# Key columns of the shared projection by seven-product slabs, the last ones in narrower tiles, and the key norms at the end

## The chip, the cores and the metric

The kernel runs on one core of a Trainium2 chip. TensorE multiplies, VectorE and ScalarE do the elementwise work, GpSimd (POOL) issues loads that add into memory, and SyncE (SP) issues the plain loads. The metric is the device time of one execution in microseconds. The kernel before takes 1988.17 us, the median of three runs (1988.16 to 1988.75).

## The reference

Two decoder layers work on 256 tokens of width 2048, in float32. Between them the kernel makes keys and values that the second layer reads:

```python
kv = rms_norm(x, kv_norm) @ w_kv                     # 2048 x 3072
k1, k2 = kv[..., :768], kv[..., 768:1536]            # two maps of 12 heads x 64
v = kv[..., 1536:]                                   # 12 heads x 128
k1 = partial_rope(rms_norm(k1, k_norm), cos, sin)    # the norm is per head
k2 = partial_rope(rms_norm(k2, k_norm), cos, sin)
```

Each layer also attends to a memory of 256 rows, `mkv = rms_norm(mem, mem_norm[i]) @ w_mem_kv[i]`, with 512 key and 512 value columns. Ahead of the keys and values stands layer 0's feed-forward block, behind them the second layer's input projection (its queries) and the differential attention.

## The kernel before

**Products in three passes.** Float32 operands are split into a rounded high part and a low rest, and a product is high x high, low x high and high x low: three matmuls. Activations are split once for each chunk of 128 features (`split_gain`, line 432: ScalarE writes the high part, VectorE the low one). Weights are split block by block as they come (`Feed._split`, line 190): ScalarE casts a block of 512 columns into one of six slots of `hi_ring` (line 195), VectorE subtracts into the same slot of `lo_ring` (line 198).

**The feed.** A first dry pass of the program writes down the order of all weight blocks; the second pass loads them in that order. A "narrow" job is one such block of 128 x 512. Before TensorE's work of a job is issued, `fill` (line 245) prepares up to three jobs beyond it (`AHEAD`), and loads run a few loads further ahead (`load`, line 129) on the SP queue, into four buffers "raw" of two jobs each (line 138). The instructions of each engine run in order. An engine can also start on instructions that are ready early, so that VectorE and ScalarE may be as far ahead of TensorE as the six slots allow.

**Slabs.** A slab is a pair of feature chunks by 1024 columns, that is a 2 x 2 arrangement of blocks, multiplied with a 2 x 2 arrangement of x (two chunks by two halves of the tokens) by the seven-product scheme of Strassen and Winograd. Each of seven PSUM banks gathers one product over all eight slabs. The left half of the slab is loaded into a tile "slab", the right half beside it; sums of its blocks are made by two adds of VectorE (lines 224 and 238) and by two loads on the POOL queue that add into memory (`add_right`, line 167). A slab has four jobs, which use six, three, six and six matmuls of 512 columns; VectorE makes low halves of 1024, 512, 1024 and 1024 columns for them. The matching sums of x are made by `kv_sums` (line 1588) for each pair of chunks: four VectorE operations of 128 columns, a cast, and a subtraction (line 1605). When a product is complete, `close` (line 1630) combines the banks by two ScalarE copies and seven VectorE adds.

**The clock of the emission.** The program counts ticks: each 128 x 512 job of the tiles ticks once, slab jobs do not. `at(d, fn)` (line 329) puts work `d` ticks later, so other work is spread between the tiles' steps by hand.

**The stage.** After layer 0's feed-forward block the order on TensorE is:
- Three key tiles of 512 columns (`map_tile`, line 500, 16 steps of six matmuls of 512 columns by `wide_step`, line 477). Behind each stand its norms (`key_rows`, line 555: two copies and two squares on ScalarE; two reductions, two multiplications and small operations on VectorE), its rotation (`rope`, line 608) and, nine ticks later, its transposition into `kT` (`turn_rows`, line 635).
- Four tiles of 256 columns on the single bank "st": two for the last 512 value columns, two for the memory's values (`half_step`, line 505: two feature chunks, twelve matmuls of 256 columns). From the second on the slabs of the first 1024 value columns stand between the half steps (`kv_slabs`, line 1612; 26 jobs on 19 half steps once it has begun).
- The memory's key tile (`mk1`, line 1747) with the last two slab jobs. After its seventh step `end` lets the other work go on, and the splits of `x_mx` for the queries are put on the following 16 ticks (line 1755). Behind it come the norms of the memory's keys and copies of its values.
- The query tiles (line 1888), the first of which needs chunk n of `x_mx` at its step n.

Beside this run the squares of the residual (`later_square`, line 747, ticks 2 to 9), the column scales (`columns`, tick 12), the loads of the memory (`mem_again`, line 1558, ticks 8, 17, 26 and 35, into the "raw" buffers of the weights) with four splits each, five to eleven ticks later, and `kv_sums` at ticks 12, 18, ... 54. The chunks of `x_kv` become ready at the end of the feed-forward block; chunk 7 is its last.

Of the kernel before, what the change touches and what calls it, by code (L numbers as in the profile page):

```python
# [311 lines left out]
def program(ctx, tc, plan, dry, xT, memT, par, lam, cst, wst, yT):  # L312
# [192 lines left out]
    def half_step(ps, w, l, c, k, xs):  # L505

        hi, lo = feed.quad([(w, l, k, c, 2), (w, l, k + 1, c, 2)])
# [127 lines left out]
    def turn_rows(raw, i, dst, g, low=None):  # L635


        t4 = pp.tile([P, 2, T], F32, tag="ot"[i // 2 % 2], bufs=1, name="tr")
# [928 lines left out]
    for p in range(4):  # L1567
        at(8 + 9 * p, lambda p=p: mem_again(p))
# [13 lines left out]

    def mv_place(h, n, t):

        four = x_kv[:, 4 * h + 2 * t : 4 * (h + n - 1) + 2 * t + 1 : 4, :]
        return four[:, :, P:T], four[:, :, T + P : 2 * T]
# [22 lines left out]
    for i in range(8):  # L1609
        at(12 + 6 * i, lambda i=i: kv_sums(i))  # L1610

    def kv_slabs():
# [3 lines left out]
        last_v = []  # L1616
# [3 lines left out]
        out = {}  # L1620
# [9 lines left out]
        def close(j):  # L1630
            if j == 0:
                one = tp.tile([P, 2, 512], F32, tag="rows", bufs=3, name="v_a")
                two = tp.tile([P, 2, 512], F32, tag="rows", bufs=3, name="v_b")
                out.update(u=one[:, 0, :], c11=one[:, 1, :], v=two[:, 0, :], c12=two[:, 1, :])
                nc.scalar.copy(out["u"], banks[0])
                add(out["c11"], out["u"], banks[1])
            elif j == 1:
                nc.scalar.copy(out["v"], banks[2])
            elif j == 2:
                u, v, c12 = out["u"], out["v"], out["c12"]  # L1640
                add(u, u, banks[3])
                sub(c12, v, u)
                add(c12, c12, banks[4])
            else:
                u, v = out["u"], out["v"]
                add(u, u, banks[5])
                sub(v, v, u)
                add(u, u, banks[6])
                for k, (c, t, x) in enumerate(
                    ((0, 0, out["c11"]), (1, 0, out["c12"]), (1, 1, v), (0, 1, u))  # L1650
                ):
                    at(1 + k // 2, lambda c=c, t=t, x=x: scale(c, t, x))
# [4 lines left out]
        def run(n, i, j):  # L1657
# [18 lines left out]
            if i == 7:  # L1676
                close(j)
# [3 lines left out]
            for p in range(-1, 9)  # L1681
            for j, i in enumerate((p + 1, p, p, p - 1))
            if 0 <= i < 8
        ]
        slab = {}

        def some(n):
            for _ in range(n):
                i, j = jobs.pop(0)
                if j == 0:  # L1690
                    slab[i] = feed.slab(
                        [
                            [("w_kv", 0, 2 * i, c, 4), ("w_kv", 0, 2 * i + 1, c, 4)]
                            for c in (3, 4)
                        ]
                    )
                run(slab[i], i, j)

        for h in range(4):
            bank = pp.tile([P, 512], F32, tag="st", bufs=1, name="mv1" if h > 1 else "v1")  # L1700
            for q in range(8):
                n = 8 * h + q
                some(0 if n < 9 else 1 if n < 13 else (26 * (n - 12) + 9) // 19 - (26 * (n - 13) + 9) // 19)
                if h < 2:
                    half_step(bank, "w_kv", 0, 10 + h, 2 * q, x_kv)
                else:
                    half_step(bank, "w_mem_kv", 1, h, 2 * q, mems1)
            if h == 0:
                last_v += [tp.tile([P, 512], F32, tag=g, bufs=1, name="v_c") for g in ("acc2", "rowsq")]
            for t in range(2):  # L1710
                two = bank[:, T * t : T * t + T]
                if h < 2:
                    nc.scalar.activation(
                        last_v[t][:, T * h : T * h + T], two, AF.Copy, scale=c1[0][:, t : t + 1]
                    )
                else:
                    two = two.rearrange("p (h d) -> p h d", h=2)
                    split_rows(*mv_place(2 * h - 4, 2, t), two, mem_c[0][:, t : t + 1])
# [298 lines left out]
```

## Time and profile before

| what | value |
|---|---|
| median of three runs | 1988.17 us |
| the profiled execution | 1988.15 us |
| its span, first to last instruction | 1986.4 us |
| TensorE, VectorE, ScalarE, POOL busy | 100%, 91%, 79%, 12% |
| mean granted TensorE clock | 1.000 |
| read from HBM | 422.19 MB, 214 GB/s over the span |

A row of a group reads: line, engine, operation, tile written and tiles read, shapes, count | busy us, mean ns of one | idle time of the engine just before, and what ended it. A row of the timeline begins with start and duration in us. PE is TensorE's matmuls, PEld its weight loads, DVE is VectorE, ACT ScalarE, POOL GpSimd, SPq SyncE's queue.

### The profile page before, as it was taken

To read this page: it belongs to the slowest core of one execution; us is meant where nothing else is said; L and a number is where in the kernel's file an instruction comes from. 1 tells how busy PE (TensorE), PEld (TensorE's weight loads), DVE (VectorE), ACT (ScalarE), POOL (GpSimd) and SP (SyncE) were. 2 spreads that over 40 slices of the span, in tenths; PEclk is the share of its full clock that TensorE was granted. 3 is DMA by queue.
4 is the path that set the end of the run, shared out by engine and by line. 5 is a ranking of instruction groups with operands and counts; after the bars stand their busy time and mean duration, and the time that the engine had idled before them with its cause. 6 is when DMAs were issued, how large, how long until landed. Compare 5 with 4: busy or idle time off the path is not lost.

```text
span 1986.4 us, 32353 instructions
## 1 busy us (share of the span) xinstructions
PE 1982.2 (100%) x10554; PEld 1696.7 (85%) x10554; DVE 1799.4 (91%) x3317; ACT 1566.1 (79%) x2894; POOL 235.3 (12%) x277
## 2 busy tenths in 40 slices
PE   9999999999999999999999999999999999999999
PEld 8888888888888888888898889888888888888888
DVE  8888889999999999889878798989999999999888
ACT  7766677788878888778757799777788888888775
POOL 0000011111111111110011000001111111111110
PEclk9999999999999999999999999999999999999999
DMA  9555578888888888765776534568888888988875
GB/s 316 180 184 198 189 201 236 238 228 234 237 227 236 232 231 231 216 192 193 236 210 204 178 128 139 193 194 231 233 236 230 234 236 224 242 229 229 229 208 146
DMA packets 149929, 426.41 MB, mean 215 GB/s; under 512 B 16896, under 2 KB 19584, under 8 KB 149760
## 3 DMA queue, kind: packets, MB, share of 16 engines
q1 hardware_dynamic: 110448, 353.03, 53.5%
q0 software_dynamic: 39168, 71.32, 21.5%
q8 instruction: 82, 1.34, 0.3%
q14 instruction: 87, 0.71, 0.1%
q10 hardware_dynamic: 144, 0.01, 0.0%
HBM read 422.19 MB, written 2.10 MB: 214 GB/s over the span
## 4 chain that ended last, share of the span: by engine, by line
PE 100%; ACT 0%; DVE 0%; issue 0%
PE x_bank L456 22%; PE x_bank L458 11%; PE p L948 10%; PE p L950 10%; PE p L951 10%; PE wo L456 6%; PE wo L458 3%; PE u L456 2%; PE ff L456 1%; PE u L458 1%; PE q L490 1%; PE k L490 1%; PE q L492 1%; PE q L491 1%; PE k L492 1%; PE k L491 1%
## 5 line engine op out<-in xcount | busy, mean ns | idle before, releaser
L195 ACT CAST hi_ring<-raw 128x512 fp32r<-128x512 f32 x905 | 551.4, 619 | 165.5 <-PE x_bank L456 40.1
L198 DVE TENSOR_TENSOR lo_ring<-raw,hi_ring 128x512 fp32r<-128x512 f32 x905 | 610.2, 686 | 49.2 <-ACT hi_ring L195 42.9
L456 PE MATMUL x_bank<-fx,hi_ring 128*128 128x512 f32 x1728 | 540.1, 394 | 0.0
L458 PEld LDWEIGHTS x_bank<-fx,lo_ring 128*128 128x128 f32 x1728 | 324.5, 188 | 73.5
L198 DVE TENSOR_TENSOR lo_ring<-room,hi_ring 128x1024 fp32r<-128x1024 f32 x256 | 312.6, 1222 | 43.1 <-ACT hi_ring L195 41.6
L195 ACT CAST hi_ring<-room 128x1024 fp32r<-128x1024 f32 x256 | 269.4, 1052 | 95.9 <-PE x_bank L456 44.0
L458 PE MATMUL x_bank<-fx,lo_ring 128*128 128x256 f32 x1728 | 339.5, 278 | 0.0
L456 PEld LDWEIGHTS x_bank<-fx,hi_ring 128*128 128x128 f32 x1728 | 286.3, 189 | 26.0 <-ACT room L835 1.5
L198 DVE TENSOR_TENSOR lo_ring<-slab,hi_ring 128x1024 fp32r<-128x1024 f32 (+1 forms) x272 | 259.4, 954 | 40.2 <-ACT hi_ring L195 36.3
L195 ACT CAST hi_ring<-slab 128x1024 fp32r<-128x1024 f32 (+1 forms) x272 | 224.1, 834 | 61.1 <-PE p L950 28.0
L170 POOL DMA_DIRECT2D slab<-in_w x136 | 117.6, 864 | 1199.9 <-DVE lo_ring L198 1193.6
L948 PE MATMUL p<-hi_ring,sit 128*128 128x512 f32 x480 | 188.3, 392 | 0.0
L950 PE MATMUL p<-hi_ring,sit 128*128 128x512 f32 x480 | 187.4, 391 | 0.0
L951 PE MATMUL p<-lo_ring,sit 128*128 128x512 f32 x480 | 186.6, 389 | 0.0
L170 POOL DMA_DIRECT2D room<-in_w x128 | 110.5, 864 | 485.8 <-DVE lo_ring L198 467.9
L456 PE MATMUL wo<-cat,hi_ring 128*128 128x512 f32 x512 | 161.6, 397 | 0.0
L948 PE MATMUL p<-hi_ring,z 128*128 128x512 f32 x368 | 145.2, 394 | 0.0
L950 PE MATMUL p<-hi_ring,z 128*128 128x512 f32 x368 | 143.8, 391 | 0.0
L951 PE MATMUL p<-lo_ring,z 128*128 128x512 f32 x368 | 143.4, 390 | 0.0
L458 PEld LDWEIGHTS wo<-cat,lo_ring 128*128 128x128 f32 x512 | 95.9, 188 | 22.3
L951 PEld LDWEIGHTS p<-lo_ring,sit 128*128 128x128 f32 x480 | 90.1, 188 | 19.7
L948 PEld LDWEIGHTS p<-hi_ring,sit 128*128 128x128 f32 x480 | 90.0, 187 | 13.1
(464 smaller groups left out, 3671.1 us busy)
## 6 DMA issues: line engine op xcount, KB each, us to landing
raw<-in_w SPq DMA_DIRECT2D x450, 512.0 KB, 4.3
slab<-in_w SPq DMA_DIRECT2D x136, 512.0 KB, 5.7
slab<-in_w POOLq DMA_DIRECT2D x136, 256.0 KB, 5.4
room<-in_w SPq DMA_DIRECT2D x128, 256.0 KB, 4.6
room<-in_w POOLq DMA_DIRECT2D x128, 256.0 KB, 5.5
memraw<-in_mem SPq DMA_DIRECT2D x5, 512.0 KB, 4.7
resid<-in_x SPq DMA_DIRECT2D x8, 256.0 KB, 5.6
out_y<-resid SPq DMA_DIRECT2D x16, 128.0 KB, 1.9
```

The lines of the kernel that those rows point to most:

```text
L170: self.nc.gpsimd.dma_start(t, self.wst[h, :, 0:512], accum_op=ALU.add)
L195: self.last_cast = self.nc.scalar.copy(hi, src)
L198: low = self.nc.vector.tensor_sub(lo, src, hi.bitcast(F32))
L456: nc.tensor.matmul(ps, hi, xs[:, k, :], start=first and c == 0, stop=False)
L458: nc.tensor.matmul(ps[:, T : 2 * T], lo, xs[:, k, 0:T], start=False, stop=last and c == len(ks) - 1,)
L490: nc.tensor.matmul(ps[t], x[t][1], hi, start=k == 0, stop=False)
L491: nc.tensor.matmul(ps[t], x[t][0], hi, start=False, stop=False)
L492: nc.tensor.matmul(ps[t], x[t][0], lo, start=False, stop=k == NK - 1)
L948: nc.tensor.matmul(ps, a[1], hi, start=new, stop=False, **again)
L950: nc.tensor.matmul(ps, a[0], hi, start=False, stop=False, **again)
L951: nc.tensor.matmul(ps, a[0], lo, start=False, stop=end, **again)
```

## The change

It makes one sequence of sixteen slabs: eight for the first 1024 value columns, then eight for the first 1024 key columns, over the same seven banks and the same sums of x. The last 512 key columns come first, as two tiles of 256 columns on "st"; then the last values, then the memory's values. That makes 48 half steps in the place of 48 wide steps and 32 half steps. The slab jobs start at the fifth half step, one for each of six half steps, then 54 on 38; four are left for the memory's key tile. The norms of the last key tile stand at half step 16 (`last_keys`, on raw columns whose scale is put in afterwards), its transposes at half step 24 on bank "st". The products of the values wait in `kv`, and are scaled into `vv` at the end; the key products are combined into "rows" tiles, and `key_rows`, `rope` and the transposes of those two key tiles come 4 to 15 ticks after `end`, which is now called after the eighth step of the memory's key tile. The memory's values wait in four small tiles and are split after that tile. `kv_sums` moves to ticks 1, 5, 8, ... 23, the memory loads to ticks 8, 13, 18 and 23.

```diff
-    def half_step(ps, w, l, c, k, xs):
+    def half_step(ps, blocks, k, xs):
-        hi, lo = feed.quad([(w, l, k, c, 2), (w, l, k + 1, c, 2)])
+        hi, lo = feed.quad(blocks(k) + blocks(k + 1))
...
     for p in range(4):
-        at(8 + 9 * p, lambda p=p: mem_again(p))
+        at(8 + 5 * p, lambda p=p: mem_again(p))
...
     for i in range(8):
-        at(12 + 6 * i, lambda i=i: kv_sums(i))
+        at(2 + 3 * i if i else 1, lambda i=i: kv_sums(i))
+    c1 = []
+    def last_keys(raw):
+        v = tp.tile([P, 16], F32, tag="w16", bufs=6, name="kv")
+        for t in range(2):
+            sq = tp.tile([P, 512], F32, tag="rowsq", bufs=1, name="ksq")
+            nc.scalar.activation(sq, raw[:, t, :], AF.Square, scale=0.125)
+            nc.vector.tensor_reduce(
+                out=v[:, 8 * t : 8 * t + 8], in_=sq.rearrange("p (h d) -> p h d", d=64),
+                axis=AX.X, op=ALU.add,
+            )
...
+            nc.vector.tensor_mul(rows, rows, yb)
+        rope(raw, ktab)
+    def turn_keys(c, i, rows, tag=None):
+        turn_rows(rows, 2 * i, kT[:, 4 * c + 2 * i : 4 * c + 2 * i + 2, :], gcol(G_KN), tag=tag)
...
-        def close(j):
+        def close(g, j):
+            o = (out, keys)[g]
             if j == 0:
...
+                if g:
+                    one = tp.tile([P, 2, 512], F32, tag="rows", bufs=3, name="k_a")
+                    two = tp.tile([P, 2, 512], F32, tag="rows", bufs=3, name="k_b")
...
         jobs = [
             (i, j)
-            for p in range(-1, 9)
+            for p in range(-1, 17)
             for j, i in enumerate((p + 1, p, p, p - 1))
-            if 0 <= i < 8
+            if 0 <= i < 16
         ]
...
+        counts = [0] * 4 + [1] * 6
+        for n in range(38):
+            counts.append((54 * (n + 1) + 9) // 38 - (54 * n + 9) // 38)
+        for n, x in ((16, 2), (24, 3)):
+            while counts[n] < x:
+                m = next(m for m in (n + 2, n - 2, n + 4, n - 4, n + 3, n - 3) if counts[m] == 2)
+                counts[m] -= 1
+                counts[n] += 1
...
+        for h in range(6):
+            left = counts[8 * h]
+            if h == 2:
+                some(1)
+                left -= 1
+                c1.extend(columns("x"))
+                last_keys(k_rows)
+            elif h == 3:
+                for i in range(2):
+                    some(1)
+                    left -= 1
+                    turn_keys(2, i, k_rows, "st")
+            some(left)
+            bank = pp.tile([P, 512], F32, tag="st", bufs=1, name=("k1", "v1", "mv1")[h // 2])
             for q in range(8):
...
+                if q:
+                    some(counts[8 * h + q])
+                half_step(bank, kinds[h], 2 * q, x_kv if h < 4 else mems1)
...
         def end():
...
+                at(1, lambda t=t: nc.scalar.copy(vv[2][:, t, :], last_v[t]))
+            for k, (c, t, x) in enumerate(((0, 0, "c11"), (0, 1, "u"), (1, 0, "c12"), (1, 1, "v"))):
+                at(2 + k // 2, lambda c=c, t=t, x=x: scale(c, t, out[x]))
+            def rows_of(c):
+                x = key_rows([keys[n] for n in (("c11", "u"), ("c12", "v"))[c]], c1, 64)
+                rope(x, ktab)
+                for i in range(2):
+                    at(7 + i, lambda i=i: turn_keys(c, i, x))
+            at(4, lambda: rows_of(0))
+            at(7, lambda: rows_of(1))
...
-    c1 = []
-    at(12, lambda: c1.extend(columns("x")))
-    for c in range(3):
-        ps = pair_of_banks(c, "k1")
-        map_tile(ps, "w_kv", 0, (2 * c, 2 * c + 1, 6 + 2 * c, 7 + 2 * c), x_kv)
-        rows = key_rows(ps, c1, 64)
-        rope(rows, ktab)
...
     for k in range(NK):
-        if k in (2, 6):
+        if k in (1, 3, 5, 7):
             one_of_slabs(1)
         wide_step(ps, ("w_mem_kv", 1, k, 0, 4), mems1, k)
-        if k == 6:
+        if k == 7:
             end_of_slabs()
...
+    at(9, mem_values)
+    at(11, mem_keys)
```

More of the change, by code (lines that the diff above doesn't have):

```diff
@@ L1644, in close @@
             else:
[L1645 removed]
+                u, v = o["u"], o["v"]
                 add(u, u, banks[5])
@@ L1699, in kv_slabs @@
[L1699 to L1708 removed]
+                            blocks_of(g, 2 * i, c) + blocks_of(g, 2 * i + 1, c)
```

124 lines of the change are left out of this document (69 added, 55 removed).

## The prediction

> **What bounds the kernel now.** I read the page first: the span, the busy shares and the chain of work that ended last.
>
> ```profile
> span 1986.4 us, 32353 instructions
> PE 1982.2 (100%) x10554; PEld 1696.7 (85%) x10554; DVE 1799.4 (91%) x3317; ACT 1566.1 (79%) x2894; POOL 235.3 (12%) x277
> PE 100%; ACT 0%; DVE 0%; issue 0%
> ```
>
> The chain is TensorE from end to end, so a matmul saved is time saved as long as the other engines keep it fed. VectorE at 91% is the one with the least room: it makes the low half of every weight block. The stage that is changed runs from 919.8 (first key matmul) to 1095.6 us (first query matmul). I cut it with the windows view; columns are PE, PEld, DVE, ACT, POOL busy us with counts, clock, DMA share, GB/s.
>
> ```profile
> 430.00:830.00 400.00, 400.00 (x2038) 339.08 (x2037) 374.63 (x588) 336.76 (x563) 71.97 (x84) 1.00 0.86 231
> 919.80:987.30 67.50, 67.50 (x311) 56.10 (x310) 63.67 (x162) 57.16 (x123) 0.00 (x0) 1.00 0.65 216
> 919.80:940.00 20.20, 20.20 (x94) 16.78 (x93) 20.16 (x53) 19.49 (x47) 0.00 (x0) 1.00 0.59 195
> 999.30:1071.30 72.00, 71.94 (x451) 63.98 (x450) 55.53 (x72) 45.59 (x65) 13.34 (x16) 1.00 0.80 220
> 1071.30:1095.60 24.30, 24.30 (x109) 20.13 (x108) 23.26 (x43) 21.25 (x43) 0.00 (x0) 1.00 0.69 217
> 919.80:1095.60 175.80, 175.74 (x966) 152.17 (x965) 152.17 (x299) 130.99 (x243) 13.80 (x16) 1.00 0.71 216
> ```
>
> The reader is to see that VectorE is busy 152.17 of 175.8 us here, that in the first 20.2 us it has 0.04 us of rest while TensorE goes on without a gap, and that the long feed-forward stretch (430 to 830) lives with VectorE at 374.63 of 400. So VectorE may be full for a while, because it works ahead of TensorE; it may not be overfull for longer than that lead. The granted clock is 1.00 throughout.
>
> **The matmuls.** Recorded matmul ends are modelled, so I price by start-to-start distance in the timeline: key tile, 256-column half step, slab products.
>
> ```profile
> 919.91 0.40 PE L490 MATMUL k<-hi_ring,x_kv 128*128 128x512 f32 x1
> ...
> 924.00 0.39 PE L490 MATMUL k<-hi_ring,x_kv 128*128 128x512 f32 x1
> ...
> 987.51 0.28 PE L516 MATMUL v<-hi_ring,x_kv 128*128 128x256 f32 x1
> ...
> 988.94 0.28 PE L516 MATMUL v<-hi_ring,x_kv 128*128 128x256 f32 x1
> ...
> 1034.22 0.40 PE L1626 MATMUL vp<-hi_ring,kv_sums 128*128 128x512 f32 x1
> ...
> 1035.61 0.28 PE L516 MATMUL mv<-hi_ring,mems 128*128 128x256 f32 x1
> ```
>
> Eighteen key matmuls lie between the first pair (16 steps of 6 a tile): 4.09 / 18 = 0.227 us. Twelve 256-column ones lie between the second: 1.43 / 12 = 0.119. Six slab products between the third: 1.39 / 6 = 0.231.
>
> The change removes two of the three key tiles, 2 x 96 = 192 matmuls: 192 x 0.227 = 43.6 us. It adds eight slabs of 21 (seven products of three passes): 168 x 0.231 = 38.8. That is -4.8. The last 512 key columns go from 96 wide matmuls (21.8 us) to 192 narrow ones (192 x 0.119 = 22.8): +1.0. Together **-3.7 us**. Bounds: slab products at the key tiles' 0.227 would make it -4.5; as far above their own 0.231 (0.235) -3.1. Key transposes keep their number and only move, 16 of them into the query stage.
>
> The Trainium skill ("TensorE: Matmul & The Clock Gate", Back-to-back issue gap) puts an isolated warm matmul at N / 2.4 + 2.5 ns, 216 ns for 512 columns and 109 for 256; by that the narrow tiles would cost nearly nothing extra, the matmuls would come to about -4.9 and the whole to 1.2 us less than my sum. The trace has 227 and 119 here, so I do not use it.
>
> **VectorE, the first half.** Here the cost lies. Consecutive operations overlap a little, so I take what a run of them costs:
>
> ```profile
> 904.67 3.71 DVE L198 TENSOR_TENSOR lo_ring<-raw,hi_ring 128x512 fp32r<-128x512 f32 x6
> L198 DVE TENSOR_TENSOR lo_ring<-vv,hi_ring 128x1024 fp32r<-128x1024 f32 x12 | 14.7, 1224 | 4.7 <-ACT hi_ring L195 4.6
> L238 DVE TENSOR_TENSOR vv<-vv,slab 128x512 f32<-128x512 f32 x6 | 4.1, 686 | 0.0
> L349 DVE SCALAR_TENSOR_TENSOR mems<-memraw,param,mems 128x256 fp32r<-128x256 f32 x16 | 7.6, 478 | 1.9 <-ACT mems L433 1.9
> L755 DVE TENSOR_TENSOR acc<-acc,later 128x256 f32<-128x256 f32 x10 | 4.2, 421 | 0.0
> L566 DVE TENSOR_REDUCE kv<-ksq 128x8 f32<-128x512 f32 x6 | 4.1, 680 | 0.0
> L1601 DVE TENSOR_TENSOR kv_f<-kv_a,kv_f 128x128 f32<-128x128 f32 x8 | 2.3, 287 | 0.1
> L615 DVE TENSOR_TENSOR rb<-krow,krope 128x64 f32<-128x64 f32 x6 | 1.3, 215 | 0.0
> 924.03 0.62 ACT L195 CAST hi_ring<-raw 128x512 fp32r<-128x512 f32 x1 [0.51 <-PE k L491]
> ```
>
> Six low halves of 0.69 us take 3.71: 0.60 each, so 0.08 of each recorded time lies under the next. Less 0.08, the 1024-wide low half is 1.14, other 512-wide operations (adds, reductions) 0.60, the 256-wide split 0.40, the plain 256-wide add 0.34, the 128-wide one 0.20, the 64-wide 0.13. The last row says how far ahead VectorE and ScalarE can be: a cast waits for TensorE's key step, so all six ring slots (SLOTS) are taken then; for narrow jobs that is a lead of up to six.
>
> One slab costs VectorE three 1024-wide low halves, one 512-wide and two adds: 3 x 1.14 + 3 x 0.60 = 5.2 us, against 4 x 0.60 = 2.4 for the same columns as tiles. Eight more: +22.5 us; the closing sums of the key products, seven at 0.60: +4.2. So some 27 us are added to a VectorE that had 23.6 to spare, in a stage that is to get shorter.
>
> How it is spread decides. Up to half step 24 (the second half of the last values) the new order asks TensorE for 24 x 12 x 0.119 = 34.3 us and 29 slab jobs; the jobs have 153 matmuls, 35.3 us; with 12 transposes and column sums at 0.11 (an estimate: half the 0.227 of a wide one) 70.9 us. Before that half step can start, VectorE must have done the following. Low halves of half steps: 25 are needed, six stand in the ring at 919.8, and 19 x 0.60 = 11.4. Slab jobs: 22 wide low halves, 7 narrow ones and 14 adds, 25.1 + 12.6 = 37.7. All eight column sums of x, which were spread over ticks 12 to 55 and now are over ticks 1 to 24: 8 x (4 x 0.20 + 0.60) = 11.2. The squares of the residual: ten adds, 3.4. Leftovers of the feed-forward stage: six 256-wide splits of x_kv and three adds, 3.4. The last key tile and the column scales: four 512-wide operations, a rotation of 1.3 and about 1.1 in small ones, 4.8. About eight of the sixteen memory splits, whose loads now start five ticks apart: 3.2. One closing sum: 0.6.
>
> Together 75.7 us against 70.9: VectorE is overfull by **4.8 us**, on TensorE's path, since the lead is already in the sum. Later it is not: from half step 32 on the slabs alone ask of VectorE about 0.8 of TensorE's time (in 999.3 to 1071.3, 55.53 of 72), but time lost is not got back. Bounds: if the memory splits, which nothing needs before half step 32, are let behind, 1.6; if the six slots hide still more than I counted, 0; if VectorE can only be filled as in the feed-forward stretch (374.63 of 400), 75.7 / 0.937 = 80.8, that is 9.9. I take 4.8, since the row 919.8 to 940 shows VectorE filled to 20.16 of 20.20.
>
> Within it lies a small wait: the last chunk of x_kv. The half steps eat two chunks at 1.43 us, where the tiles ate one in 1.36.
>
> ```profile
> 925.53 0.48 DVE L349 SCALAR_TENSOR_TENSOR x_kv<-resid,param,x_kv 128x256 fp32r<-128x256 f32 x1
> ```
>
> Chunk 7 is ready at 926.0; half step 3 wants it at 919.9 + 3.5 x 1.43 = 924.9. That is 1.1 us of TensorE's wait, in which VectorE goes on, so it is part of the 4.8 and not added.
>
> **Bank, queues, end.** The single bank "st" now also takes the column sums and two pairs of transposes at half steps 16 and 24, and it changes hands twice more among the tiles; each time the next matmul waits for ScalarE to empty it, with the rest of TensorE's queue behind. A slab job (0.7 or 1.4 us) stands between most of them.
>
> ```profile
> L644 ACT ACTIVATE kv<-tr,param 128x512 f32<-128x512 f32 x6 | 3.8, 685 | 0.0
> PEld v L516 <- ACT v_c L1713: 0.3, 1, 0.3
> PEld mv L516 <- ACT v_c L1713: 0.4, 1, 0.4
> ```
>
> The emptying takes 0.69; the two handovers of now that show a wait have 0.3 (no job between) and 0.4. Three of the new ones fall into the overfull stretch, where a wait of TensorE gives VectorE time. I take nothing; five of 0.4, 2.0, are the upper end. POOL's accumulating loads double to 32; in 430 to 830 84 of POOL's instructions went by with TensorE full, so nothing. The four scalings and copies at the end are ScalarE's, beside TensorE.
>
> The key norms of the first two tiles now come behind the slabs. From step 8 of the memory keys to step 8 of the queries, 16 steps of 6 x 0.227 = 21.8 us, VectorE has 16 low halves (9.6), 16 splits of x_mx (6.4), two key tiles (four 512-wide, rotation, small ones: 4.1 each, 8.2), the memory rows (2.8) and three closing sums (1.8): 28.8, over by 7.0. Six slots at 1.36 are a lead of 8.2, and the slabs before leave room to build it. So nothing, with 7.0 if there is no lead.
>
> **Sum.** The profiled execution took 1988.15 us (its span 1986.4 and 1.75 around it), against the median 1988.17. 1988.15 - 3.7 + 4.8 = **1989.3 us**. A difference of 0.2%, 4.0 us, is about what a measurement tells from no change.
>
> **The rivals.**
>
> *VectorE hides it all.* The ring and the order let the memory splits and the squares slip behind, and TensorE never waits: 1988.15 - 3.7 = 1984.4, or 1983.6 at the lower end of the matmuls. For it: the first 20.2 us of now, full and without a gap. Against it: a demand of 75.7 in 70.9 that lasts three times as long. Chance 0.20, half of it beyond 4.0 us.
>
> *The end is overfull (slower).* The key norms at the end meet x_mx and the memory rows; ScalarE too is at 21.25 of 24.3 us there. It decides from the point where the lead at memory-key step 8 is under 7.0 us: with only the three jobs that AHEAD prepares, 4.1 us, the queries' first steps wait 2.9, with none 7.0. On top of the forecast 1992.2 to 1996.3. For it: the norm's chain goes to ScalarE and back, in which VectorE idles. Against it: half steps 32 to 47 leave VectorE a fifth of its time. Chance 0.27.
>
> *Memory loads hold the weight buffers.* Each holds one of four "raw" buffers for eleven ticks; at five ticks apart three are held at once about ticks 18 and 23, and the SP queue's next weight load stands behind, with every slab load ordered after it.
>
> ```profile
> raw<-in_w SPq DMA_DIRECT2D x450, 512.0 KB, 4.3
> ```
>
> One landing exposed is 4.3 us: 1993.6. For it: the order of loads is forced. Against it: one buffer lasts two half steps with their jobs, longer than a landing. Chance 0.08.
>
> The Trainium skill ("Perfetto Trace Analysis", Identifying the Most-Contended Engine) would work on the engine with the highest occupancy, and by its measures that is VectorE (91%) before TensorE's weight loads (85%); it speaks against a change that gives VectorE 27 us. The present trace has TensorE as the chain nevertheless, so I let it weigh only through the sums above.
>
> **How the numbers follow.** Forecast 0.45, with its own range 1986.1 (memory splits deferred) to 1994.4 (VectorE filled to 0.937); about a fifth of that lies over 1992.1. Faster by over 0.2%: half of the first rival, 0.10. Slower: the second rival 0.27, a little over half of the third and the upper part of the forecast: 0.37. Within: 0.53. The range from 1984.0 to 1996.5 leaves out a little of the first rival and of the second with everything against it.
>
> **What would show it.** Right: in the changed profile 336 slab products and 384 + 192 narrow matmuls; VectorE at 99% from the stage's start to about half step 24; TensorE waiting there for low halves by 4 to 5 us in total, and hardly later; a wait of about 1 us for x_kv near its fourth half step. Wrong: no wait of TensorE for low halves before half step 24 (the first rival); waits of several us at the first query steps (the second); casts that wait for raw loads (the third); or slab products for keys spaced over 0.24.

## The result, and the profile after

The changed kernel takes 2000.23 us (median of four runs, 1998.4 to 2001.23), the kernel before 1988.46 us on the same chip (1988.16 to 1989.17). The ratio is 1.0058 with a 95% interval of 1.004 to 1.0075: it is slower by 11.8 us, not by the 1.2 us that were forecast. The profiled execution took 2001.23 us.

The first part of the page of the changed kernel, and its chain of waits:

```profile
span 1999.4 us, 32560 instructions
PE 1986.2 (99%) x10626; PEld 1698.4 (85%) x10626; DVE 1824.9 (91%) x3343; ACT 1576.8 (79%) x2898; POOL 249.1 (12%) x293
PE 96%; DVE 2%; DMA 1%; ACT 0%; issue 0%; DVEq 0%
```

TensorE was the whole chain before; now VectorE has 2% and the DMA 1% of it. The shares of the page alone would not show this change: 99% and 91% are nearly what they were. The windows view does (columns as in the prediction: PE, PEld, DVE, ACT, POOL busy, granted clock, DMA share, GB/s). The stage now runs from 919.6 to 1106.6; 1005.0 and 1018.7 are the starts of half steps 24 and 28.

```profile
430.00:830.00 400.00, 400.00 (x2039) 339.08 (x2038) 374.70 (x589) 336.47 (x563) 71.67 (x83) 1.00 0.87 232
919.60:940.00 20.40, 19.15 (x129) 16.88 (x128) 18.13 (x36) 16.37 (x35) 3.45 (x4) 1.00 0.64 182
940.00:1005.00 65.00, 59.69 (x335) 49.37 (x335) 62.06 (x124) 48.31 (x83) 10.35 (x12) 0.97 0.80 216
1005.00:1018.70 13.70, 11.25 (x64) 9.55 (x63) 10.11 (x16) 6.57 (x12) 1.73 (x2) 0.88 0.75 214
1018.70:1106.60 87.90, 87.90 (x499) 76.90 (x499) 77.52 (x115) 64.22 (x103) 12.08 (x14) 1.00 0.77 220
919.60:1106.60 187.00, 177.99 (x1022) 152.69 (x1021) 167.82 (x288) 135.48 (x232) 27.61 (x32) 0.98 0.76 214
```

The stretch 430 to 830 is as it was. The stage has grown from 175.8 to 187.0 us, and from 1018.7 on TensorE is full again: within the stage all of the loss lies in the first 99 us. (Behind the stage the span is 2.0 us longer, since 16 transposes moved there.) There TensorE stands idle for 1.25 + 5.31 + 2.45 = 9.0 us, and the clock of 0.97 and 0.88 takes up to 3.6 more (an estimate: 0.03 x 65 + 0.12 x 13.7). The rest hides in short gaps: a recorded matmul lasts 0.39 us where the next one starts after 0.23, so a gap of 0.16 doesn't count as idle.

VectorE is idle there too: 2.27 + 2.94 + 3.59 = 8.8 us. An engine that is overfull and idle at once is waiting in order behind something. Three places show for what. At the first slab VectorE waited for a load that adds into memory, and ScalarE waited for weights, longest just before 1010 (waits view of the changed kernel; the three numbers are sum, times and longest):

```profile
DVE vv L224 <- DMA slab<-in_w: 2.1, 1, 2.1
ACT hi_ring L195 <- DMA raw<-in_w: 6.3, 3, 3.7
```

The SP queue and ScalarE around that second place (timeline of the changed kernel):

```profile
1000.07 0.33 SPq L1560 DMA_DIRECT2D memraw<-in_mem  x1
1002.41 0.33 SPq L156 DMA_DIRECT2D raw<-in_w  x1
...
1009.66 1.14 ACT L195 CAST hi_ring<-raw 128x512 fp32r<-128x512 f32 x2 [3.68 <-DMA raw<-in_w]
```

The memory's load is issued at 1000.07; the weights behind it in the same queue go out at 1002.41 and are there at 1009.66, 7.2 us later. The SP queue's own waits say why so late: that load had stood for up to 8.7 us at the head of the queue, for a buffer that an earlier memory tile still held.

```profile
SPq L1560 <- DVE mems L349: 10.5, 2, 8.7
```

The third place is half step 16, where the norm of the last key tile stands (timeline of VectorE, then of TensorE):

```profile
975.41 0.37 DVE L1627 TENSOR_SCALAR ky<-ky,c_x 128x8 f32<-128x8 f32 x2
975.68 1.29 DVE L1632 TENSOR_TENSOR kv<-kv,ky 128x512 f32<-128x512 f32 x2
976.89 0.28 DVE L614 TENSOR_TENSOR ra<-kv,krope 128x128 f32<-128x128 f32 x1
...
978.04 0.69 DVE L198 TENSOR_TENSOR lo_ring<-raw,hi_ring 128x512 fp32r<-128x512 f32 x1
```
```profile
975.71 0.39 PE L1656 MATMUL vp<-hi_ring,x_kv 128*128 128x512 f32 x1
978.78 0.58 PE L519 MATMUL v<-lo_ring,x_kv 128*128 128x256 f32 x1 [2.68 <-DVE lo_ring L198]
979.16 0.41 PE L516 MATMUL v<-hi_ring,x_kv 128*128 128x256 f32 x1
...
981.29 0.41 PE L518 MATMUL v<-hi_ring,x_kv 128*128 128x256 f32 x1
```

The low half that TensorE needs comes at 978.04, behind 2.6 us of norm and rotation. And the twelve matmuls behind the gap are slow: ten distances from 979.16 to 981.29 are 0.213 us each instead of 0.119.

### The profile page after: what moved, and what is told of

It reads as the page before. It is cut to its first block, busy times and chain, and to the rows that moved or that the text cites. A ratio compares the mean times of both kernels' runs of the same rounds, so it can differ in the third digit from the quotient of the medians.

```text
span 1999.4 us, 32560 instructions
## 1 busy us (share of the span) xinstructions
PE 1986.2 (99%) x10626; PEld 1698.4 (85%) x10626; DVE 1824.9 (91%) x3343; ACT 1576.8 (79%) x2898; POOL 249.1 (12%) x293
## 4 chain that ended last, share of the span: by engine, by line
PE 96%; DVE 2%; DMA 1%; ACT 0%; issue 0%; DVEq 0%
PE x_bank L456 22%; PE x_bank L458 11%; PE p L948 10%; PE p L950 10%; PE p L951 10%; PE wo L456 6%; PE wo L458 3%; PE u L456 2%; PE ff L456 1%; PE u L458 1%; PE q L492 1%; PE vp L1655 1%; PE q L490 1%; PE vp L1656 1%; PE q L491 1%; PE vp L1657 1%
## 5 line engine op out<-in xcount | busy, mean ns | idle before, releaser
L195 ACT CAST hi_ring<-raw 128x512 fp32r<-128x512 f32 x873 | 532.0, 619 | 174.9 <-PE x_bank L456 39.7
L198 DVE TENSOR_TENSOR lo_ring<-raw,hi_ring 128x512 fp32r<-128x512 f32 x873 | 588.5, 686 | 48.2 <-ACT hi_ring L195 42.6
L198 DVE TENSOR_TENSOR lo_ring<-slab,hi_ring 128x1024 fp32r<-128x1024 f32 (+1 forms) x288 | 274.7, 954 | 34.1 <-ACT hi_ring L195 31.2
L195 ACT CAST hi_ring<-slab 128x1024 fp32r<-128x1024 f32 (+1 forms) x288 | 237.0, 834 | 57.5 <-PE p L950 26.1
L170 POOL DMA_DIRECT2D slab<-in_w x144 | 124.4, 864 | 1160.0 <-DVE lo_ring L198 894.2
```

Of the source, the lines that this page charges most:

```text
L170: self.nc.gpsimd.dma_start(t, self.wst[h, :, 0:512], accum_op=ALU.add)
L195: self.last_cast = self.nc.scalar.copy(hi, src)
L198: low = self.nc.vector.tensor_sub(lo, src, hi.bitcast(F32))
```

## The experiments

Theory A was the prediction's step, more work for VectorE up to half step 24 than TensorE's time there. Theory B was its third rival, the memory's loads that hold weight buffers and stand in the queue ahead of weights. All times are medians. Each is given with its ratio to the kernel before, measured beside it, and the 95% interval of the ratio. The loss of the changed kernel is 11.8 us.

**One memory tile at a time** (e1_mem_one).

```diff
-                5 + 2 * k,
+                4 + k,
-        at(8 + 5 * p, lambda p=p: mem_again(p))
+        at(10 + 7 * p, lambda p=p: mem_again(p))
```

> The changed kernel with the four memory tiles loaded at ticks 10, 17, 24 and 31 and split four to seven ticks later, so that no two of them hold weight buffers at once; nine splits still fall before half step 24, as eight or nine do now. Theory A (VectorE has more work in the first half than TensorE lasts): VectorE's work there stays the same, 1999 to 2001 us. Theory B (weight loads wait on the SP queue for buffers that the memory tiles hold): the late loads after half step 24 go, 1989 to 1995 us, and no wait of a cast for a raw load over 2 us is left between the first key step and the queries.

1998.21 us, ratio 1.0052 (1.0035 to 1.0069): 2 us better than the changed kernel, below A's range and above B's. ScalarE now waited for the memory tiles themselves (5.6 us in four waits up to 1040).

**No buffer held** (e2_no_hold).

```diff
-        t = wp.tile([P, 4, T], F32, tag="raw", bufs=4, name="memraw1")
-        nc.sync.dma_start(t, memT[:, 4 * p : 4 * p + 4, :])
+        t = kv[:, 2048:3072].rearrange("p (k t) -> p k t", k=4)
+        if p == 0:
+            nc.sync.dma_start(t, memT[:, 0:4, :])
```

> The changed kernel with one memory tile loaded in place of four, into an unused part of the key tile, and all sixteen splits made from it at the ticks of now; left out are three loads and the memory's true content. VectorE and ScalarE have the work of now, no weight buffer is held. Theory A: 1999 to 2001 us. Theory B: 1988 to 1994 us. A result between says how much of the 11.5 us either one has.

1994.51 us, 1.003 (1.0019 to 1.0042): 5.7 us better. The same 100 us of the changed kernel, and then of this one:

```profile
920.00:1020.00 100.00, 90.99 (x532) 76.66 (x531) 90.31 (x174) 71.90 (x129) 15.52 (x18) 0.97 0.76 210
```
```profile
920.00:1020.00 100.00, 95.24 (x582) 82.78 (x582) 98.32 (x186) 77.30 (x137) 17.30 (x20) 0.98 0.78 214
```

VectorE's idle time falls from 9.7 to 1.7 us, with no operation of VectorE less. So most of that idle time came with the memory's loads, and they have about half of the loss; the time is close to B's range, not within it. Three loads are left out here as well, so this run alone cannot tell the held buffers from the loads themselves; e5 below keeps them.

**No norm at half step 16** (e3_no_norm).

```diff
                 c1.extend(columns("x"))
-                last_keys(k_rows)
```

> The changed kernel without the norms and the rotation of the last 512 key columns at half step 16; their transposes stay. Left out are the scaling and the rotation of a third of the keys, some 4.8 us of VectorE. Theory A: VectorE is overfull there, so all of it comes off TensorE's path, and the gap of 2.83 us near half step 16 with it: 1993 to 1996 us. Theory B: the loads set the pace, at most 1.5 us: 1998.5 to 2001 us.

1995.53 us, 1.0034 (1.0021 to 1.0047): 4.7 us better for 4.8 us of work. The gap near half step 16 is gone. Window 970 to 980 of the changed kernel, then of this one:

```profile
970.00:980.00 10.00, 6.90 (x35) 5.42 (x34) 10.00 (x32) 4.40 (x7) 0.86 (x1) 0.93 0.54 118
```
```profile
970.00:980.00 10.00, 10.00 (x62) 8.87 (x62) 10.00 (x19) 5.95 (x8) 1.80 (x3) 1.00 0.89 244
```

VectorE is full in both, with 32 operations in the first, many of them the small ones of the norm, and 19 in the second. The time lies in A's range: this block cost its full price.

**Slab jobs spread** (e4_pace).

```diff
-        counts = [0] * 4 + [1] * 6
-        for n in range(38):
-            counts.append((54 * (n + 1) + 9) // 38 - (54 * n + 9) // 38)
+        counts = [0] * 8 + [1] * 16
+        for n in range(24):
+            counts.append((44 * (n + 1) + 9) // 24 - (44 * n + 9) // 24)
```

> The changed kernel with the slab jobs spread otherwise: none in the first eight half steps, one a step in the next sixteen (two at half step 16), 43 on the last 24; the sums of x at ticks 2, 6, 9, 13, 16, 19, 21 and 24. The memory's loads stay. Theory A: up to half step 24 VectorE then has about 56 us of work and TensorE 55, where it was 75.7 and 70.9, so nearly all of the loss goes: 1984.5 to 1988 us. Theory B: the weights asked for per tick fall in the first half but rise behind it, while the memory tiles hold as many buffers: 1991 to 1998 us.

2003.54 us, 1.0077 (1.0062 to 1.0092): 3.3 us worse, a miss for both. ScalarE's queue near half step 24 shows the price (timeline):

```profile
994.19 1.30 ACT L433 ACTIVATE mems<-memraw,param 128x256 fp32r<-128x256 f32 x3 [1.92 <-DMA memraw<-in_mem]
995.40 0.81 ACT L1775 ACTIVATE v_c<-v,c_x 128x256 f32<-128x256 f32 x2
```

The emptying of the single bank (L1775) stands behind splits that wait for a memory tile, and TensorE's transposes wait 3.0 us for the bank. My reading is that with fewer slab jobs the ticks pass faster, so that the memory's load, set in ticks, comes too late for its split. It fits that in e6, where the memory lies elsewhere, the same spreading costs only 0.1 us beside e5.

**Memory tiles in the key tile** (e5_mem_in_keys: three of them, ticks 2, 6 and 17; e6_keys_pace: the same with the spread jobs).

```diff
+        else:
+            t = kv[:, place : place + 1024].rearrange("p (k t) -> p k t", k=4)
```

> The changed kernel, whole, with the first three memory tiles loaded into parts of the key tile that are unused before half step 24, at ticks 2, 6 and 17, and split at ticks 10 to 23, and only the fourth in a weight buffer, at tick 28. Theory B (held buffers make loads late): as without held buffers, 1993 to 1996 us. Theory A (VectorE's sum alone): twelve splits instead of nine before half step 24, 1.2 us more work, so 2000 to 2002 us. If both hold, B's gain less that: 1994.5 to 1997 us.

> The same loads of the memory, and besides the slab jobs spread as in the run before that lost time by it (none in eight half steps, one a step in sixteen, 43 in 24). If that run lost because the memory's loads waited behind the weights and ScalarE waited for them, with the emptying of the bank behind it, the spreading now gains: 1985 to 1990 us, and the waits of ScalarE for memory tiles are gone. If the spreading is bad by itself (slab jobs at nearly two a half step ask more of VectorE than they give TensorE): 1996 us or more.

1999.14 us (1.0052, 1.0037 to 1.0067) and 1999.25 us (1.0054, 1.0038 to 1.0071). The first lies between the cases, the second where the spreading is bad by itself. In the 100 us shown for e2, e5 does nearly as well, with all loads kept and more splits in that stretch:

```profile
920.00:1020.00 100.00, 94.45 (x572) 81.13 (x571) 95.98 (x181) 76.26 (x134) 16.41 (x20) 0.98 0.78 216
```

TensorE's idle time is 5.6 us, against 9.0 in the changed kernel and 4.8 in e2; VectorE's is 4.0, against 9.7 and 1.7. So the larger part of e2's gain there does not come from the three loads that it left out. But near 1063 e5 loses 3.6 us of its own, idle time and half clock together: the load of a slab's left half stood 6.3 us at the head of the SP queue for its own buffer, until 1051.66, and the weights behind it, issued up to 1053.13, reached ScalarE only at 1062.83, after it had waited 3.7 us. No memory tile was held any more then. In e6 most of its loss falls on 960 to 1000: VectorE is full up to 990, and then come the transposes on the single bank.

**Both left out** (e7_both_out, the edits of e2 and e3).

> The changed kernel with one memory tile loaded in place of four and without the norms of the last key columns: both leave-outs of before together (left out are three loads, the memory's true content, and the scaling and rotation of a third of the keys). Alone they gave 5.7 and 4.7 us. If the two causes are separate, 10.4 us: 1989 to 1991 us. If both only fill up one common reserve, less: 1992 to 1994.5 us; if one makes room for the other, down to 1985 us, near the 1984.4 that matmuls alone would give.

1991.08 us, 1.0012 (1.0002 to 1.0021): 9.1 us better, against 10.4 by adding, and just above the first range. The two causes are nearly separate.

**All four tiles in the key tile** (e8_mem_keys4), **small sums on POOL** (e9_sums_pool), **both** (e10_keys4_pool). In e8 and e10 two tiles are loaded over others before their last splits, so part of the memory is another one's; the operations are as many.

```diff
-        nc.vector.tensor_sub(s1, a21, a22)
+        nc.gpsimd.tensor_sub(s1, a21, a22)
```

> The changed kernel, whole, with all four memory tiles loaded into the unused parts of the key tile (ticks 1, 2, 10 and 14) and split at ticks 7 to 22, so that none of them ever holds a weight buffer. If the held buffers cost what the run with one memory tile suggests (5.7 us), less the seven splits that come before half step 24 now (2.8 us): 1995 to 1998 us, and the late load that cost 3.6 us behind half step 32 when the fourth tile lay in a weight buffer is gone. If that run gained by the three loads it left out: 1999 to 2002 us.

> The changed kernel, whole, with the four small sums of each of the eight column sums of x (32 operations of 128 columns) on POOL in place of VectorE. Theory A: 32 x 0.20 = 6.4 us of VectorE's work leave the first half, and all of it comes off TensorE's path: 1993 to 1996 us. If POOL, whose loads wait for VectorE, gives the sums late, or if the held buffers alone set the pace: 1998 us or more.

> Both: memory tiles in the key tile and the small sums on POOL. If the two causes add up as the leave-outs did: 1988 to 1992 us. If the gaps that are left come from somewhere else (the first slab's accumulating load, the single bank): 1993 us or more.

2002.3 us (1.0067, 1.0052 to 1.0082), 2010.14 us (1.0109, 1.0094 to 1.0124) and 2002.93 us (1.0073, 1.0056 to 1.009). The repair of B alone missed, and the relief of VectorE cost 10 us where A had it gain 6; e9 and e10 lie in their second cases. In e8 all sixteen splits come before half step 24. Two stretches of the changed kernel, then the same two of e8, show that what it gained late it lost early:

```profile
920.00:970.00 50.00, 48.00 (x300) 41.31 (x299) 46.35 (x88) 42.16 (x82) 8.62 (x10) 1.00 0.78 221
990.00:1020.00 30.00, 26.09 (x141) 20.83 (x140) 24.66 (x40) 20.08 (x33) 4.31 (x5) 0.94 0.74 197
```
```profile
920.00:970.00 50.00, 45.29 (x277) 39.59 (x275) 43.60 (x83) 40.08 (x78) 7.76 (x9) 0.97 0.77 221
990.00:1020.00 30.00, 28.53 (x170) 23.76 (x169) 28.81 (x47) 19.53 (x29) 5.60 (x7) 1.00 0.83 227
```

From 990 to 1020 TensorE's idle time falls from 3.9 to 1.5 us, and the clock is 1.00; up to 970 it rises from 2.0 to 4.7. One early wait: ScalarE stood 2.8 us before a memory tile, until 969.21, with the emptying of the single bank behind it, and TensorE's column sums waited 2.6 us for that bank. In e9 ScalarE waited for POOL's sums (waits view), with the weights' casts behind them:

```profile
ACT kv_sums L1599 <- POOL kv_f L1596: 14.5, 5, 4.7
```

**The repaired kernel** (e11_repair): the whole computation. Half of the memory's tiles go into the key tile at ticks 2 and 6, half into small tiles from tick 25 on; the last key rows lie in the third part of the key tile, are normed at half step 40 and turned at the end. With the spread of jobs: e12_repair_pace.

```diff
-        k_rows = kv[:, 1024:2048].rearrange("p (t c) -> p t c", t=2)
+        k_rows = kv[:, 2048:3072].rearrange("p (t c) -> p t c", t=2)
...
-                last_keys(k_rows)
-            elif h == 3:
-                for i in range(2):
-                    some(1)
-                    left -= 1
-                    turn_keys(2, i, k_rows, "st")
+            elif h == 5:
+                last_keys(k_rows)
...
+            at(2, turn_last)
```

> The changed kernel, whole and with its own counts of slab jobs, but without the two causes: the first two memory tiles go into parts of the key tile unused before half step 24, the other two, from tick 25 on, into the small tiles that the sums of x have left, so no weight buffer is held and eight splits come before half step 24; and the last key columns lie in the third part of the key tile, are normed and rotated at half step 40 and turned at the end, in two free banks. If VectorE's work and its idle time up to half step 24 are the cause, it does as well as with both left out (1991.1 us): 1989.5 to 1992.5 us. If the norm only moves its price behind half step 40, or the leave-outs gained by what they left out: 1994 to 1998 us.

> The same, and the slab jobs spread (none in eight half steps, one a step in sixteen, 43 in 24). If only VectorE's sum up to half step 24 counts, it is now below TensorE's: 1985 to 1989 us, below the kernel before. If the slab buffers, and with them the load queue that all weights share, set the pace of the slabs behind half step 24, where they then come at nearly two a half step: 1993 us or more.

1991.2 us (1.0013, 1.0004 to 1.0022) and 1992.24 us (1.002, 1.0011 to 1.0029). The first lies in its first range, where both leave-outs together were, with nothing left out. Its 100 us, and the window of half step 16:

```profile
920.00:1020.00 100.00, 98.77 (x613) 86.16 (x612) 97.75 (x171) 79.61 (x137) 18.16 (x21) 1.00 0.84 230
...
970.00:980.00 10.00, 10.00 (x62) 8.83 (x62) 10.00 (x18) 6.84 (x11) 1.73 (x2) 1.00 1.01 274
```

TensorE's idle time falls from 9.0 to 1.2 us, and the clock is 1.00. This execution took 1988.74 us and was the fastest of eleven; the median is 2.5 us longer, so its trace shows fewer waits than most of the runs had. The spread of the jobs brings nothing: 1992.24 lies between its two cases.

**The start of the slabs** (e13_start8, e14_start6, e15_start8_late): the repaired kernel with other counts, such as

```diff
+        counts = [0] * 8 + [1] * 4
+        for n in range(36):
+            counts.append((56 * (n + 1) + 9) // 36 - (56 * n + 9) // 36)
```

> The repaired kernel (no weight buffer held by the memory, the last key norms at half step 40) with the first slab job at half step 8 in place of 4, one job for each of four half steps, then 56 on 36; sums of x at ticks 2, 6, 9, 12, 15, 17, 20 and 23. In the repaired kernel about 3 us of TensorE's waits lie at 927 to 945 us, where the first slab's load and its accumulating load are late; in the kernel that began at half step 8 and came at nearly two a half step behind half step 24 they were gone, but 3 us of others stood behind half step 20. If the start is the remaining cause, the first go and the others do not come: 1986.5 to 1989 us. If VectorE's sum decides, the order of slab jobs changes nothing: 1990 to 1992.5 us.

> The same with the first slab job at half step 6, one for each of six half steps, then 54 on 36, and the sums of x at the changed kernel's own ticks. If the start is the cause, some of the 3 us goes: 1987.5 to 1990 us. If VectorE's sum decides: 1990 to 1992.5 us.

> The same with the first slab job at half step 8, one for each of eight half steps, then 52 on 32 (1.6 a half step). Between the two before: if the waits behind half step 20 come from the density of slab jobs there, some of them show: 1988 to 1990.5 us; if only the start counts, as the run with 56 on 36: 1986.5 to 1989 us.

1993.74 us (1.0027, 1.0015 to 1.0038), 1992.82 (1.0023, 1.0014 to 1.0032) and 1990.42 (1.0012, 1.0004 to 1.0021). The waits at 927 to 945 went (where the slabs start at half step 8, 1.1 us for the last chunk of x_kv came), but the time did not fall: e13 lies above both of its ranges, e14 just above its second, e15 within its first. In e13 one wait of another kind, near 1007, took their place (waits view, 995 to 1016):

```profile
PE vp L1667 <- ACT hi_ring L195: 4.9, 1, 4.9
ACT mems L433 <- DMA memraw<-in_mem: 4.7, 1, 4.7
```

ScalarE stands before a memory tile that has not landed, the casts behind it, and TensorE behind those.

**VectorE's work in the repaired kernel** (e16_no_small_sums, e17_no_squares).

```diff
-        nc.vector.tensor_sub(s1, a21, a22)
-        nc.vector.tensor_sub(s3, a11, a21)
-        nc.vector.tensor_sub(s2, s1, a11)
-        nc.vector.tensor_add(s4, a12, s2)
```
```diff
-        nc.vector.tensor_add(acc["x"], acc["x"], sq)
+        if n == 15:
+            nc.vector.tensor_add(acc["x"], acc["x"], sq)
```

> The repaired kernel (1991.2 us) without the four small operations of VectorE in each of the eight column sums of x; ScalarE writes the two scaled chunks into their place. Left out are the sums that the slab scheme needs: 32 x 0.20 = 6.4 us of VectorE. If VectorE's sum as such is what remains, nearly all of the loss goes: 1984.5 to 1987 us. If it is the loads and the slab buffers: 1989 us or more.

> The repaired kernel without the adds of the residual's squares but one; the squares are still made on ScalarE. Left out are nine or more adds of 0.34 us, so 3.1 to 3.4 us of VectorE between ticks 2 and 9, and with them the true column scales. If VectorE's sum is what remains: 1987.5 to 1989 us. If work so early lies beside waits for the first slab's loads and costs nothing: 1990 to 1992 us.

1989.55 us (1.0005, 0.9997 to 1.0014) and 1990.45 us (1.0009, 1.0 to 1.0018): beside e11, 6.4 us of work are worth 1.7 us by the medians, and 3.3 us are worth 0.8. Each kernel's own runs scatter by about 4 us, so neither gain is clear of the scatter. Both times lie in the second cases: VectorE's work in the repaired kernel is not on the path at its full price.

**Memory loaded earlier before its splits** (e18_early_loads, on e15).

```diff
+    for d, a, n, place in ((2, 0, 4, 0), (6, 4, 4, 1024), (26, 8, 4, None), (28, 12, 2, None), (34, 14, 2, None)):
+        at(d, lambda a=a, n=n, place=place: mem_load(a, n, place))
```

> The repaired kernel with its slab jobs begun at half step 8 (one for each of eight half steps, then 52 on 32), which took 1990.42 us, and with the memory's second half loaded at ticks 26, 28 and 34 and split five to ten ticks later, where it was split four ticks after its load. In that run ScalarE waited up to 4.2 us near 980 us for a memory tile, with the casts of weights queued behind it. If such waits are what remains, they go: 1986.5 to 1989 us, at or below the kernel before. If not: 1990 to 1992 us as without it.

1991.15 us (1.0012, 1.0003 to 1.0021): the second case, no gain against e15. In the profiled execution, the slowest of its eleven runs, the largest wait was now that of the single bank, at 984:

```profile
PEld v L516 <- ACT v_c L1775: 2.8, 1, 2.8
```

## Why the prediction was wrong, step by step

**The matmuls: right.** Three rows of the changed kernel's timeline give the new spacing:

```profile
1043.37 0.28 PE L516 MATMUL mv<-hi_ring,mems 128*128 128x256 f32 x1
...
1044.80 0.40 PE L1655 MATMUL vp<-hi_ring,x_kv 128*128 128x512 f32 x1
...
1046.87 0.28 PE L516 MATMUL mv<-hi_ring,mems 128*128 128x256 f32 x1
```

Twelve narrow ones in 1.43 us are 0.119 each, nine slab products in 2.07 are 0.230, as forecast. So 1988.15 - 3.7 = 1984.4 us is what is left without waits, and the medians put 2000.2 - 1984.4 = 15.8 us of waits where the prediction had 4.8.

**VectorE, the first half: this is the step that failed.** Its work was counted nearly rightly. The largest groups of low halves from 919.5 to 1000 in the changed kernel:

```profile
L198 DVE TENSOR_TENSOR lo_ring<-raw,hi_ring 128x512 fp32r<-128x512 f32 x21 | 14.4, 687 | 2.0 <-ACT hi_ring L195 1.9
L198 DVE TENSOR_TENSOR lo_ring<-vv,hi_ring 128x1024 fp32r<-128x1024 f32 x9 | 11.0, 1220 | 0.0
L198 DVE TENSOR_TENSOR lo_ring<-slab,hi_ring 128x1024 fp32r<-128x1024 f32 x8 | 9.8, 1221 | 0.7 <-ACT hi_ring L195 0.6
...
L198 DVE TENSOR_TENSOR lo_ring<-kv,hi_ring 128x1024 fp32r<-128x1024 f32 x4 | 4.9, 1222 | 0.4 <-ACT hi_ring L195 0.4
L198 DVE TENSOR_TENSOR lo_ring<-slab,hi_ring 128x512 fp32r<-128x512 f32 x7 | 4.8, 686 | 0.0
```

Twenty-one wide low halves (22 forecast up to half step 24), seven narrow ones (7), 21 of half steps (19). What failed is "I take 4.8, since the row 919.8 to 940 shows VectorE filled to 20.16 of 20.20": the step from the excess of a sum to the wait. That row stood in key tiles, with 16 narrow low halves from one kind of buffer beside the squares and four memory splits; no slab and no norm shared its queue. In the changed order VectorE was idle for 8.8 of 99 us and still late. Half step 24 began at 1005.0 instead of 919.6 + 75.7 = 995.3: up to there VectorE was busy for 18.13 + 62.06 = 80.2 us and idle for 5.2, so besides the idle time it did some 4.5 us of work that the sum did not ask for by then (four low halves of half steps and two memory splits more, among others). The upper bound of the same step (0.937 full, 9.9 us) was too low as well.

The runs without an excess show the same. In e7 and e11 the norm is gone from the first half, nearly all of a term of 4.8 us. By the prediction's prices VectorE then needs about 71 us there, no more than TensorE, and the sum would give about 1984.4 us. They took 1991.1 and 1991.2. With 6.4 us of work less (e16) it was still 1989.6.

**The third rival: it was there, and priced too low.** It had a chance of 0.08 and one landing, 4.3 us. Its wait at the head of the queue was 8.7 us. What the memory's tiles cost as they lie in the changed kernel is 5.7 us by e2, which leaves three loads out as well, and 4.3 by the repaired kernel (9.0 less the 4.7 of the norm). Its own sign came too: casts waited 6.3 us for raw loads. The argument "one buffer lasts two half steps, longer than a landing" left out that the load waits for its buffer before it can begin, and that a landing then takes 7.2 us.

**A term that was hidden in the sum: the norm at half step 16.** In the sum its 4.8 us happen to equal the whole excess. It cost 4.7 (e3). In the trace it does so at one place, as a block of in-order work between the ring and one low half, and not as a share of a sum over 76 us. That the place decides, and not the amount, is argued from the trace: no run put as much other work there.

**The rest of the steps.** The x_kv wait of 1.1 us was 0.2 here, because TensorE had nine products of the first slab in its place, from 924.66 on; with a later start of the slabs it was 1.1 as forecast. The single bank, taken at nothing with 2.0 as the upper end, showed waits of 3.0 and 2.8 us in e4 and e18: the emptying is short, but it stands in ScalarE's queue behind others. The end was not overfull: TensorE is full from 1018.7 to 1106.6, and idle for only 0.13 of the 43.4 us behind, where the queries begin, so the second rival falls. That time lost is not got back was right, but loss went on behind half step 24, by 2.45 us of idle time and a lower clock up to 1018.7.

**What stays open.** Of the 15.8 us the runs assign 9.0 to the norm and the memory's tiles (e11), and by the medians 1.7 of what is left to 6.4 us of VectorE's work (e16). Some 5 us remain. In the profiles they are the first slab's loads, the x_kv chunk, ScalarE before a memory tile, or the single bank, one or two at a time; where one was moved, another took its place, so no single cause of the rest is shown. The memory's share is not split exactly between the held buffers and the place of the splits: e5 and e8, which freed buffers and split earlier, gained where the held buffers had cost, and lost nearly all of it elsewhere, e5 to a slab's buffer and e8 to early splits. No version tried is faster than the kernel before.

## What to carry to other kernels

A sum of an engine's work gives its load, but not that it can be filled: ask of each wait in front of it what stands behind the waiting instruction, in its queue and in the load queue. When two works share a queue or a buffer with the weights, move the one that nobody needs soon (here the memory's tiles and one norm: 9 of 11.8 us), before reckoning with the sum. A saving of 3.7 us on the busiest engine was worth less here than the waits that it opened, where the next engine had no room left for some 70 us.

## What the runs showed of the hardware

**The clock can fall after a gap of 2.7 us.** The stretch behind the gap of half step 16 in the changed kernel:

```profile
979.00:982.00 3.00, 3.00 (x14) 2.90 (x15) 3.00 (x4) 0.90 (x2) 0.00 (x0) 0.50 0.75 259
```

The granted clock is 0.50 there. The ten distances of 0.213 us in place of 0.119 alone cost 0.9 us, on top of the gap of 2.68. The Trainium skill ("TensorE: Matmul & The Clock Gate", What's actually happening) puts the half rate behind an idle window of about 3.4 us. Here it came after a shorter idle time, and the measurement decides. The length of the gap alone does not tell: behind a gap of 2.06 us, up to 979.84 in e1, the clock stayed at 1.00 (first row), and in e14 it fell behind one of 1.81 and one of 0.53 us, up to 978.58 (second row).

```profile
979.00:983.00 4.00, 3.16 (x20) 2.63 (x21) 4.00 (x7) 1.24 (x2) 0.86 (x1) 1.00 0.59 199
```
```profile
978.60:981.90 3.30, 3.30 (x8) 2.62 (x9) 3.30 (x6) 2.17 (x6) 0.86 (x1) 0.50 0.57 194
```

So a wait of about 2 us can cost more than itself, and need not.

**POOL and VectorE slow each other.** In e9, beside POOL's sums (first fence), VectorE's low half of 512 columns took 0.95 us instead of 0.69 (second fence):

```profile
950.29 1.44 POOL L1595 TENSOR_TENSOR kv_f<-kv_f,kv_a 128x128 f32<-128x128 f32 x1
951.80 0.79 POOL L1596 TENSOR_TENSOR kv_f<-kv_a,kv_f 128x128 f32<-128x128 f32 x1
```
```profile
951.33 0.95 DVE L198 TENSOR_TENSOR lo_ring<-raw,hi_ring 128x512 fp32r<-128x512 f32 x1
```

POOL's second operation took 0.79 us there. The same operation took 0.46 at 962.90, where VectorE was idle:

```profile
962.90 0.46 POOL L1596 TENSOR_TENSOR kv_f<-kv_a,kv_f 128x128 f32<-128x128 f32 x1
```

On VectorE such an operation takes 0.29. The Trainium skill ("SBUF — State Buffer", Who interferes with whom) states that a VectorE instruction with two inputs in SBUF contends with a POOL instruction that reads SBUF. This run agrees with it: both inputs of the low half lie there.

**The repaired kernel scatters more.** Its eleven runs lie between 1988.74 and 1992.93 us, 21 of the kernel before on the same chip between 1987.43 and 1989.72. It is not the time alone that does it: ten runs of e7, on another chip and with nearly the same median, lie between 1990.54 and 1991.36. Why is not shown.
